# Sets of matmuls on TensorE added behind the last sum of squares of a two-layer encoder kernel

## The chip, the core and the metric

The kernel runs on one core of a Trainium2 chip. The metric is the device time of one execution in microseconds (us), taken as the median of several runs. A profile of one execution gives the span from its first to its last instruction and, for each engine, its instructions in order of time: TensorE (PE in the rows, with its weight loads as PEld), VectorE (DVE), ScalarE (ACT), GpSimd (POOL) and SyncE (SP), whose queue issues nearly all transfers.

## What is computed

The reference is a two-layer encoder trunk on 256 tokens of width 2048. Cut to what matters here:

```python
for i in range(DEPTH):
    h = rmsnorm(x, g_mix[i]);  z = h @ w_in[i]
    ...                                   # two kinds of attention, eight heads each
    x = x + merged @ w_out[i]
    gate, up = jnp.split(rmsnorm(x, g_ffn[i]) @ w_gate_up[i], 2, axis=-1)
    x = x + (jax.nn.silu(gate) * up) @ w_down[i]
    e = p[i] @ w_ple_in[i]
    x = x + jax.nn.sigmoid(rmsnorm(x, g_ple[i]) @ w_ple_gate[i]) * e
return rmsnorm(x, g_final)
```

## The kernel before

The activations lie in the on-chip memory (SBUF) as `xT`: 128 partitions by 16 column blocks by 256 tokens, float32. A product with a weight matrix is made one column block of 128 outputs at a time. Each operand stands as two parts of reduced precision, a high and a low one: an activation block `u` is one tile of 512 columns, the high part in columns 0 to 255 and the low part in 256 to 511 (`ua` and `ub`, sixteen such tiles each), and a piece of weights is two tiles `whi` and `wlo` of up to 1024 columns, that is eight blocks of 128 by 128.

`piece` (L181) loads a piece of weights by a transfer on SP's queue into `w`, copies it to `whi` on ACT, and subtracts on DVE to get `wlo`. There are four buffers of `w` and three of `whi` and of `wlo`. `emit` (L211 and L212) then issues, for each of the blocks, a pair of matmuls with the weights as the stationary operand: the high weights against all 512 columns, and the low weights against the 256 high columns:

```python
PE.matmul(acc, hi[:, s], u, start=start, stop=False)                  # L211
PE.matmul(acc[:, T:], lo[:, s], u[:, :T], start=False, stop=stop)     # L212
```

A product runs over one or more pieces into one bank of the accumulator memory (PSUM). Four banks rotate for products (`ps_mm`), two for attention scores, and two (`ps_at`) for small things. Of the small things three matter below. `turned` makes four transposes of 128 by 128 in float32 by matmuls with an identity (L359). `norm` sums squares over the partitions by float32 matmuls whose moving operand is a single column of ones (L271). `spread` lays the two resulting scales out over the partitions by one float32 matmul of 256 columns (L280). The last column block of the whole kernel's last product uses a variant with three matmuls of 256 columns for each block (L207 to L209).

Where the weights lie matters for the change, so it is said here in bytes within a partition, read modulo 512, which is the length of one block's row of weights: the tiles `ua`, `ub` and `wlo` start at 128, and `whi` starts at 192, behind a 64-byte tile `step` that is only there to move it. So in the kernel before the low weights lie 0 bytes, and the high weights 64 bytes, past the place of the moving operand.

The order on each engine comes from a scheduler that lists instructions by the order of the program where their inputs allow it, with some orders pinned by hand (`keep_in_program_order` pins an instruction behind the one traced before it on its engine). At the end of the last layer, `R = spread(norm(sums, DM), copied=False)` makes the final scales in a bank of `ps_at`; six multiplications on DVE then scale `xT` in place, and six transfers on SP's queue (L704) write the output. Right at the start, eight matmuls of ones into a bank that is never read (L407) run ahead of the real work.

Of the kernel before, what the change touches and what calls it, by code (L numbers as in the profile page):

```python
# [13 lines left out]
F32R = mybir.dt.float32r  # L14
I32 = mybir.dt.int32
AF = mybir.ActivationFunctionType
# [3 lines left out]
P = 128  # L20
T = 256
# [15 lines left out]
PT = 8  # L37
# [15 lines left out]
def encoder(ctx, tc, x, p, positions, cols, lams, wq, wk, wv, wcq, wckv, wkr, wga, wgb,  # L53
            w_q_up, w_kn, w_v, w_bd, w_bm, w_out, w_gate, w_up, w_down, w_pin, w_pg, rope_c, out):
    nc = tc.nc
    V, A, PE = nc.vector, nc.scalar, nc.tensor
# [3 lines left out]
    wts = pool("wts")  # L60
    tmp = pool("tmp")
    stat = pool("stat")
    ps_mm = pool("ps_mm", 4, space=PSUM)
# [3 lines left out]
    def scratch(tag, bufs, n=T):  # L67
        return tmp.tile([P, n], F32, tag=tag, name=tag, bufs=bufs)

    def bank(ps=ps_at, tag="at", name="at", shape=(P, 2 * T)):  # L70
        return ps.tile(list(shape), F32, tag=tag, name=name)

    def tt(o, a, b, op):
        return V.tensor_tensor(out=o, in0=a, in1=b, op=op)  # L74
# [4 lines left out]
    def ts(o, a, s1, s2, op0, op1=ALU.bypass):  # L79
        return V.tensor_scalar(out=o, in0=a, scalar1=s1, scalar2=s2, op0=op0, op1=op1)  # L80


    ua = [const.tile([P, 2 * T], F32R, name=f"ua{j}") for j in range(NC)]
# [12 lines left out]
    xT = const.tile([P, NC, T], F32, name="xT")  # L96
# [4 lines left out]
    at = 0  # L101
# [8 lines left out]
    ident = const.tile([P, P], F32, name="ident")  # L110
    make_identity(nc, ident)
    ones = const.tile([P, P], F32, name="ones")
# [2 lines left out]
    aside = [fa(j) for j in range(5)]  # L115
    posi = aside[0][:, 0, :].bitcast(I32)
    posf = aside[0][:, 1, :]

    def tables():
        V.tensor_copy(posf, posi)  # L120
        got = []
        for i, name in enumerate("pm"):
            ang, k, r, a = (aside[j + i][:, m, :] for j in (1, 3) for m in range(2))
            ts(ang, posf, rc[:, 2 * i : 2 * i + 1], None, ALU.mult)
            ts(k, ang, 1.0 / TWO_PI, ROUND, ALU.mult, ALU.add)
            ts(k, k, ROUND, None, ALU.subtract)
            stt(r, k, -C1, ang, ALU.mult, ALU.add)
            stt(r, k, -C2, r, ALU.mult, ALU.add)
            stt(r, k, -C3, r, ALU.mult, ALU.add)
            ts(r, r, PI_IN, -PI_IN, ALU.min, ALU.max)  # L130
            stt(a, r, -1.0, r, ALU.mult, ALU.min)
            ts(a, a, math.pi / 2, None, ALU.add)
            cs = const.tile([P, T], F32, name="cos_" + name)
            sn = const.tile([P, T], F32, name="sin_" + name)
            A.activation(cs, a, AF.Sin)
            A.activation(sn, r, AF.Sin)
            ts(sn, sn, rc[:, 2 * i + 1 : 2 * i + 2], None, ALU.mult)
            got += [cs, sn]
        return got
# [74 lines left out]
    def product(src, us, whole=False):  # L214


        acc = bank(ps_mm, "mm", "mm")
        n = len(us)
        for a in range(0, n, PT):
            m = min(PT, n - a)  # L220
            hi, lo = piece(src[:, a * P : (a + m) * P], m)
            emit(acc, hi, lo, 0, us[a : a + m], a == 0, a + m == n, whole)
        return acc[:, :T] if whole else acc
# [10 lines left out]
    def joined(acc, o=None):  # L234
        t = scratch("join", 3)
        A.activation(t, acc[:, T:], AF.Copy)  # L236
        o = scratch("a", 4) if o is None else o
        tt(o, acc[:, :T], t, ALU.add)
        return o
# [7 lines left out]
    def rsqrt(src, n, eps, width):  # L247

        v, y, a = (stat.tile([P, 2 * DH], F32, tag="r" + s, name="r" + s, bufs=2)[:, :width] for s in "vya")
        ts(v, src, 1.0 / n, eps, ALU.mult, ALU.add)  # L250
        ts(y.bitcast(I32), v.bitcast(I32), -0.5, 1597463007.0, ALU.mult, ALU.add)
        for _ in range(3):
            stt(a, y, -0.5, y, ALU.mult, ALU.mult)
            tt(a, a, v, ALU.mult)
            stt(y, a, 1.5, y, ALU.add, ALU.mult)
        return y

    def square_into(acc, src, first):
        if first:
            A.activation(acc, src, AF.Square)  # L260
        else:
            sq = scratch("sq", 2)
            A.activation(sq, src, AF.Square)  # L263
            tt(acc, acc, sq, ALU.add)

    def norm(sums, n):

        s = bank()
        for j, a in enumerate(sums):
            for b in range(2):  # L270
                PE.matmul(s[:, b : b + 1], a[:, b * P : (b + 1) * P], ones[:, 0:1], start=j + b == 0, stop=j + b == len(sums))  # L271
        return rsqrt(s[:, 0:2], n, EPS, 2)

    def spread(col, copied=True):

        dg = stat.tile([P, 2, P], F32, tag="dg", name="dg", bufs=1)
        for b in range(2):
            ts(dg[:, b, :], ident, col[:, b : b + 1], None, ALU.mult)
        s = bank()
        PE.matmul(s[:, :T], ones, dg, start=True, stop=True)  # L280
        if not copied:
            return s[:, :T]
        row = stat.tile([P, T], F32, tag="row", name="row", bufs=2)
        A.activation(row, s[:, :T], AF.Copy)  # L284
        return row

    def normed(sums, one, two):

        got = [joined(one())]
        col = norm(sums, DM)  # L290
        got.append(joined(two()))
        return spread(col), col, got

    def squares():
        return stat.tile([P, T], F32, tag="ssq", name="ssq", bufs=2)

    def stream(us, gain):

        acc = squares()

        def add(c):
            split(us[c], xT[:, c, :], g(gain, c))
            square_into(acc, xT[:, c, :], c == 0)

        return acc, add
# [110 lines left out]
    for L in range(DEPTH):  # L416

        steps = values(wv[L], ua, None if L else load)
        for vd in steps:
            if L == 0 and vd is not None:  # L420
# [3 lines left out]
                with after_splits():  # L424
                    rcol = norm([sq0[0][:, j, :] for j in range(2)], DM)
                    next(steps)
                    R = spread(rcol)
                    cos_p, sin_p, cos_m, sin_m = tables()
                    lambdas()
                break  # L430
            if L:
                next(steps)
                rcol = norm([acc], DM)
                next(steps)
                R = spread(rcol)
                break
# [5 lines left out]
        for o, t in ((cr, cos_p), (sr, sin_p), (crm, cos_m), (srm, sin_m)):  # L442
            tt(o, t, R, ALU.mult)

# [17 lines left out]
        def latent(us, w, raws):  # L462
            ss = squares()
            for c in range(len(us)):
                tt(raws[c], joined(product(w[L, c], ua)), R, ALU.mult)
                square_into(ss, raws[c], c == 0)
# [55 lines left out]
        def gate(w, store, n):  # L522
            tt(store(n), joined(product(w[L, n], ua)), R, ALU.mult)

# [115 lines left out]
        acc, add = stream(ub, f"g_ffn{L}")  # L640
# [4 lines left out]

        R, _, pre = normed([acc], lambda: product(w_gate[L, 0], ub), lambda: product(w_up[L, 0], ub))
        pT, es = ua[14:], []
# [4 lines left out]
        for part, (f0, f1) in enumerate(FF_PARTS):  # L652
            for f in range(f0, f1):
                a = pre.pop(0) if pre else joined(product(w_gate[L, f], ub))
# [9 lines left out]
            if last:  # L664
                acc, add = stream(ub, f"g_ple{L}")
# [12 lines left out]
        if final:  # L678
            sums = [squares(), squares()]
# [5 lines left out]
        else:  # L685
            acc, add = stream(ua, f"g_mix{L + 1}")
        for n in range(NC):
            if final and n == NC - 1:
                a = scratch("a", 4)
                tt(a, product(w_pg[L, n], ub, True), R, ALU.mult)  # L690
            else:
                a = pre.pop(0) if pre else joined(product(w_pg[L, n], ub))
# [5 lines left out]
            add(n)  # L698

    R = spread(norm(sums, DM), copied=False)  # L700
    for n, m in ((0, 1), (1, 1), (2, 2), (4, 4), (8, 4), (12, 4)):
        o = xT[:, n : n + m, :]
        tt(o, o, R[:, None, :].to_broadcast([P, m, T]), ALU.mult)
        nc.sync.dma_start(out[:, n : n + m, :], o)  # L704
# [84 lines left out]
```

## Time and profile before

| what | us |
|---|---|
| two timed runs | 2911.41 and 2915.62 |
| their median | 2913.51 |
| the profiled execution's own time | 2910.11 |
| its span, first to last instruction | 2908.3 |
| TensorE busy within the span | 2890.7 |
| weight loads busy (beside the matmuls) | 2539.6 |
| VectorE busy | 2062.3 |
| ScalarE busy | 1524.6 |

The mean granted TensorE clock was 0.998 of full speed. In the rows, a matmul's own duration contains time in which the next one already streams, so what a matmul costs is read from the distance between the starts of successive ones, or from a stretch's length divided by the count of instructions in it. A float32 matmul that isn't a transpose leaves two records, one of the reduced type (`fp32r`, which the rows also print as f32) leaves one. Times in windows and timelines count from the start of the span.

### The profile page before, as it was taken

How to read it: one execution, taken by the hardware profiler on the slowest of the kernel's cores; microseconds unless marked ns; L12 is line 12 of the kernel's file. 1: busy time of each engine (PE TensorE's matmuls, PEld its weight loads, DVE VectorE, ACT ScalarE, POOL GpSimd, SP SyncE). 2: the span in 40 equal slices, each digit the busy share in tenths (PEclk: the TensorE clock that was granted, in tenths of full speed). 3: DMA queues.
4: the chain of work that ended last, by engine and by line, in shares of the span. 5: the costliest groups of instructions: out<-in, count | busy, mean ns of one | idle time of the engine just before them, and what ended most of it. 6: DMA issues, size and time to landing. Idle time of an engine off the chain costs nothing.

```text
span 2908.3 us, 43980 instructions
## 1 busy us (share of the span) xinstructions
PE 2890.7 (99%) x16750; PEld 2539.6 (87%) x16750; DVE 2062.3 (71%) x3529; ACT 1524.6 (52%) x2529; POOL 1.7 (0%) x9
## 2 busy tenths in 40 slices
PE   9999999999999999999999999999999999999998
PEld 7888888888888888888888888888888888888887
DVE  7897658776666666667859976687666666666676
ACT  6676545554444444454646755555444444444554
POOL 0000000000000000000000000000000000000000
PEclk9999999999999999999999999999999999999999
DMA  7554466555665566566565445666556655655664
GB/s 236 165 163 147 159 195 197 190 186 188 184 193 189 183 189 192 189 188 188 189 188 168 151 153 167 195 195 189 186 188 184 193 188 180 197 188 189 189 186 141
DMA packets 156019, 532.40 MB, mean 183 GB/s; under 512 B 16928, under 2 KB 23840, under 8 KB 155808
## 3 DMA queue, kind: packets, MB, share of 16 engines
q1 hardware_dynamic: 155376, 529.01, 57.9%
q8 instruction: 131, 2.15, 0.3%
q14 instruction: 80, 0.66, 0.1%
q10 hardware_dynamic: 432, 0.59, 0.1%
HBM read 527.43 MB, written 2.10 MB: 182 GB/s over the span
## 4 chain that ended last, share of the span: by engine, by line
PE 99%; DVE 1%; ACT 0%; DMA 0%; SPq 0%; issue 0%; DVEq 0%
PE mm L211 61%; PE mm L212 31%; PE S L341 1%; PE mmv L394 1%; PE mmv L392 1%; PE mmv L393 1%; PE at L359 0%; PE at L563 0%; PE at L620 0%; DMA w<-in_wv 0%; PE at L280 0%; DVE xT L74 0%; PE at L271 0%; DVE wlo L74 0%; ACT whi L181 0%; DVE a L74 0%
## 5 line engine op out<-in xcount | busy, mean ns | idle before, releaser
L181 ACT ACTIVATE whi<-w 128x1024 fp32r<-128x1024 f32 (+2 forms) x1029 | 1068.5, 1039 | 1311.4 <-issue 749.3
L74 DVE TENSOR_TENSOR wlo<-w,whi 128x1024 fp32r<-128x1024 f32 (+2 forms) x1029 | 1228.6, 1194 | 740.2 <-ACT whi L181 730.4
L211 PE MATMUL mm<-ub,whi 128*128 128x512 f32 x3952 | 1381.5, 394 | 0.0
L211 PE MATMUL mm<-ua,whi 128*128 128x512 f32 x3744 | 1307.8, 394 | 0.0
L212 PE MATMUL mm<-ub,wlo 128*128 128x256 f32 x3952 | 1107.7, 280 | 0.0
L212 PE MATMUL mm<-ua,wlo 128*128 128x256 f32 x3744 | 1048.5, 280 | 0.0
L211 PEld LDWEIGHTS mm<-ub,whi 128*128 128x128 f32 x3952 | 742.1, 188 | 164.5
L211 PEld LDWEIGHTS mm<-ua,whi 128*128 128x128 f32 x3744 | 702.5, 188 | 151.5
L212 PEld LDWEIGHTS mm<-ub,wlo 128*128 128x128 f32 x3952 | 749.0, 190 | 0.8
L212 PEld LDWEIGHTS mm<-ua,wlo 128*128 128x128 f32 x3744 | 708.2, 189 | 2.2 <-DVE wlo L74 0.4
L74 DVE TENSOR_TENSOR a<-mm,join 128x256 f32<-128x256 f32 x421 | 174.8, 416 | 0.3 <-ACT join L236 0.2
L236 ACT ACTIVATE join<-mm 128x256 f32<-128x256 f32 x453 | 165.9, 367 | 5.4 <-PE mm L212 5.0
L74 DVE TENSOR_TENSOR xT<-xT,mm 128x256 f32<-128x256 f32 x256 | 106.6, 419 | 48.4 <-PE mm L212 44.5
L74 DVE TENSOR_TENSOR a<-a,row 128x256 f32<-128x256 f32 x207 | 87.2, 424 | 6.6 <-ACT row L284 0.8
L74 DVE TENSOR_TENSOR a<-a 128x256 f32<-128x256 f32 x120 | 51.0, 425 | 4.0
L392 PE MATMUL mmv<-whi,ua 128*128 128x512 f32 x128 | 51.0, 399 | 2.0 <-ACT whi L181 2.0
L74 DVE TENSOR_TENSOR ua<-a,ua 128x256 fp32r<-128x256 f32 x120 | 50.1, 417 | 1.0 <-ACT ua L244 1.0
L393 PE MATMUL mmv<-whi,ua 128*128 128x512 f32 x128 | 50.5, 395 | 0.0
L244 ACT ACTIVATE ua<-a 128x256 fp32r<-128x256 f32 x120 | 48.2, 402 | 2.7 <-DVE a L74 2.6
L350 ACT ACTIVATE E<-S,nm 128x256 f32<-128x256 f32 x96 | 44.2, 470 | 5.1 <-DVE nm L80 5.0
L394 PE MATMUL mmv<-wlo,ua 128*128 128x512 f32 x128 | 46.8, 397 | 0.1
L74 DVE TENSOR_TENSOR ssq<-ssq,sq 128x256 f32<-128x256 f32 x97 | 40.5, 417 | 0.5 <-ACT sq L263 0.5
(154 smaller groups left out, 1158.9 us busy)
## 6 DMA issues: line engine op xcount, KB each, us to landing
w<-in_w_gate SPq DMA_DIRECT2D x176, 512.0 KB, 4.6
w<-in_w_up SPq DMA_DIRECT2D x176, 512.0 KB, 4.5
w<-in_w_down SPq DMA_DIRECT2D x128, 512.0 KB, 3.7
w<-in_wga SPq DMA_DIRECT2D x64, 512.0 KB, 3.8
w<-in_wgb SPq DMA_DIRECT2D x64, 512.0 KB, 4.5
w<-in_w_out SPq DMA_DIRECT2D x64, 512.0 KB, 4.2
w<-in_w_pg SPq DMA_DIRECT2D x64, 512.0 KB, 4.4
w<-in_w_down SPq DMA_DIRECT2D x64, 384.0 KB, 3.6
```

Of the source, the lines that this page charges most:

```text
L74: return V.tensor_tensor(out=o, in0=a, in1=b, op=op)
L181: last_split[:] = A.activation(hi[:, :m], w[:, :m], AF.Copy), tt(lo[:, :m], w[:, :m], hi[:, :m].bitcast(F32), ALU.subtract)
L211: PE.matmul(acc, hi[:, s], u, start=start, stop=False)
L212: PE.matmul(acc[:, T:], lo[:, s], u[:, :T], start=False, stop=stop)
L236: A.activation(t, acc[:, T:], AF.Copy)
L244: return A.activation(hi, src, AF.Copy), tt(lo, src, hi.bitcast(F32), ALU.subtract)
L341: PE.matmul(S[:, b, :], q[:, b * P : (b + 1) * P], k, start=j == 0, stop=j == len(pairs) - 1)
L350: last_exp[0] = A.activation(E[:, b, :], S[:, b, :], AF.Exp, bias=nm[:, b : b + 1], scale=scale, accum_out=sm[:, b : b + 1])
L392: PE.matmul(banks[b], xh, hi[:, s], start=a + j == 0, stop=False)
L393: PE.matmul(banks[b], xl, hi[:, s], start=False, stop=False)
L394: last_mm[:] = [PE.matmul(banks[b], xh, lo[:, s], start=False, stop=a + j == n - 1)]
```

## The change

A function `others` is added and called once, behind the last `spread` and ahead of the six multiplications that make the output. It copies the first 1024 columns of `xT` into one `whi` and one `wlo` buffer on ACT (names `sh` and `sl`). Then it runs over 64 pairs of places: eight for the high and eight for the low part, in steps of 16 elements, 64 bytes. The index is turned by one for the high part, so that `h` and `l` count the distance from the moving operand's place in steps of 64 bytes for both; `h = 1, l = 0` is the pair of places that the kernel before has. At each pair of places it runs four sets of seven pairs of matmuls in the form of L211 and L212, each into a bank that is never read, and each behind one of four kinds of other matmuls, into a bank that isn't read either:

- `quarters`: five matmuls of 256 columns with low weights
- `transposes`: four float32 transposes of 128 by 128 of `xT`
- `sums`: four float32 matmuls of one column, with `xT` as the stationary operand
- `couples`: two matmuls of 512 columns with the high weights, then two of 256 with the low ones

All these matmuls are pinned in program order on TensorE. Nothing is removed. The buffers come from the tags that are there already, so no tile of the kernel before moves.

```diff
+    def others():
+        src = xT[:, :4, :].rearrange("p c t -> p (c t)")
+        sh = wts.tile([P, PT * P], F32R, tag="whi", name="side", bufs=3)
+        sl = wts.tile([P, PT * P], F32R, tag="wlo", name="side", bufs=3)
+        for t in (sh, sl):
+            A.activation(t, src, AF.Copy)
+        keep = tc.keep_in_program_order
+        mm = lambda *a, **k: keep(PE.matmul(*a, **k))
+
+        def quarters(at, h, l):
+            for j in range(5):
+                mm(at[:, :T], sl[:, j * P : (j + 1) * P], ua[j][:, :T], start=j == 0, stop=j == 4)
+
+        def transposes(at, h, l):
+            for j in range(4):
+                keep(PE.transpose(at[:, j * P : (j + 1) * P], xT[:, j, :P], ident))
+
+        def sums(at, h, l):
+            for j in range(4):
+                mm(at[:, j : j + 1], xT[:, j, :P], ones[:, 0:1], start=True, stop=True)
+
+        def couples(at, h, l):
+            for j in range(2):
+                mm(at, sh[:, h + j * P : h + (j + 1) * P], ua[j], start=j == 0, stop=False)
+            for j in range(2):
+                mm(at[:, T:], sl[:, l + j * P : l + (j + 1) * P], ua[j][:, :T], start=False, stop=j == 1)
+
+        for h in range(8):
+            for l in range(8):
+                name = "w" + chr(97 + h) + chr(97 + l)
+                oh, ol = 16 * ((h - 1) % 8), 16 * l
+                for before in (quarters, transposes, sums, couples):
+                    before(bank(name="between"), oh, ol)
+                    acc = bank(ps_mm, "mm", name)
+                    for j in range(7):
+                        mm(acc, sh[:, oh + j * P : oh + (j + 1) * P], ua[j], start=j == 0, stop=False)
+                        mm(acc[:, T:], sl[:, ol + j * P : ol + (j + 1) * P], ua[j][:, :T], start=False, stop=j == 6)
...
     R = spread(norm(sums, DM), copied=False)
+    others()
     for n, m in ((0, 1), (1, 1), (2, 2), (4, 4), (8, 4), (12, 4)):
```

## The prediction

> **What bounds the kernel now.** I read the page's busy shares first, then its chain of work that ended last, then windows over long stretches, then the timeline of the last 20 us.
>
> ```profile
> span 2908.3 us, 43980 instructions
> PE 2890.7 (99%) x16750; PEld 2539.6 (87%) x16750; DVE 2062.3 (71%) x3529; ACT 1524.6 (52%) x2529; POOL 1.7 (0%) x9
> ...
> PE 99%; DVE 1%; ACT 0%; DMA 0%; SPq 0%; issue 0%; DVEq 0%
> ```
>
> TensorE is busy for 2890.7 of 2908.3 us, and the chain is TensorE for 99% of the span. All idle time of TensorE is 17.6 us, so matmuls that are added go onto the path at their full price, wherever they are put. Everything then hangs on the price of one pair, and that I take from stretches in which nothing but pairs run:
>
> ```profile
> 360.00:480.00 120.00, 120.00 (x708) 106.13 (x707) 81.66 (x119) 61.61 (x96) 0.00 (x0) 1.00 0.62 196
> 2200.00:2800.00 600.00, 600.00 (x3431) 527.84 (x3430) 398.16 (x585) 282.32 (x398) 0.00 (x0) 1.00 0.61 188
> ```
>
> These are windows; the second and third numbers are the length and TensorE's busy time, with the matmuls counted behind it. In the later one 600 us hold 3431 matmuls, half of them of 512 and half of 256 columns: 600 / 1715.5 = 0.3497 us a pair. In the earlier one it is 120 / 354 = 0.339 us, of the same form with its weights at the same places. So a pair has more than one speed. The timeline shows a third, behind four transposes:
>
> ```profile
> 327.58 0.60 PE L359 MATMUL at<-ident,E 128*128 128x128 f32 x4
> 327.94 0.48 PE L211 MATMUL mm<-ua,whi 128*128 128x512 f32 x1
> 328.25 0.28 PE L212 MATMUL mm<-ua,wlo 128*128 128x256 f32 x1
> 328.38 0.40 PE L211 MATMUL mm<-ua,whi 128*128 128x512 f32 x1
> 328.61 0.28 PE L212 MATMUL mm<-ua,wlo 128*128 128x256 f32 x1
> ...
> 333.32 0.40 PE L211 MATMUL mm<-ua,whi 128*128 128x512 f32 x1
> ```
>
> From the pair that starts at 328.38 to the one at 333.32 there are 14 pairs: 4.94 / 14 = 0.353 us. Same places, three prices, 0.339, 0.350 and 0.353; the speed stays with a run of pairs, and changes where other matmuls come between.
>
> **The change part by part.**
>
> **The sets.** 64 places, four sets, seven pairs: 1792 pairs. `couples` is two more pairs at each place in another order, 128. Together 1920 pairs at 0.3497 = 671.4 us. I take 0.3497 since it lies between the other two and is the mean of the longest stretch. The trace has only one pair of places for this form; for the other 63 the nearest rows are matmuls of other operands, whose weights and moving operand lie at the same place:
>
> ```profile
> 312.45 0.52 PE L341 MATMUL S<-fb,fa 128*128 128x256 f32 x3
> 312.81 0.52 PE L341 MATMUL S<-kr,fc 128*128 128x256 f32 x3
> ```
>
> Three of 256 columns in 0.36 us (312.45 to 312.81) are 0.120 each. A pair is 768 columns, three times as many: 0.360 us. So the bounds of a pair's mean over all places are 0.340 (671.4 - 18.6) and 0.360 (671.4 + 19.8).
>
> By the Trainium skill (TensorE: Matmul & The Clock Gate, section Back-to-back issue gap) a warm matmul costs N / 2.4 + 2.5 ns, 215.8 and 109.2, so 0.325 us for a pair: an estimate of 624 us for the 1920. The stretches above show 0.339 at best, so I go by them.
>
> **What goes between.** `quarters` is five matmuls of 256 columns. The nearest rows are the last product's, which has only such matmuls:
>
> ```profile
> 2892.03 0.28 PE L209 MATMUL mm<-ub,wlo 128*128 128x256 f32 x1
> ...
> 2892.38 0.28 PE L209 MATMUL mm<-ub,wlo 128*128 128x256 f32 x1
> ```
>
> From 2892.03 to 2892.38 there are three (L209, L207, L208): 0.1175 each with rounding, 320 of them 37.6 us (0.113 to 0.120 by the pairs' speeds: 36 to 38).
>
> `transposes`: in the rows of 327.58 four transposes, and what the next matmul loses, take until the start of its L212 at 328.25, 0.67 us, against 0.235 for a plain L211 step (328.38 to 328.61). So they cost 0.44, and 64 times that is 28.2 us (up to 0.49 each, 31, with rounding and one slower step).
>
> `sums`: four float32 matmuls of one column, as in `norm`:
>
> ```profile
> L271 PE MATMUL at<-ones,ssq x44: 164/250/271, 87.4 to 2895.3; 128*128 128x1 f32 x44
> L271 PE MATMUL at<-ones,fb x8: 166/250/250, 44.6 to 45.2; 128*128 128x1 f32 x8
> ```
> ```profile
> 2808.63 0.50 PE L271 MATMUL at<-ones,ssq 128*128 128x1 f32 x4
> 2808.99 0.47 PE L211 MATMUL mm<-ub,whi 128*128 128x512 f32 x1
> 2809.30 0.28 PE L212 MATMUL mm<-ub,wlo 128*128 128x256 f32 x1
> ```
>
> The 26 such matmuls of the kernel before leave 52 records (44 and 8), two each. Four records with what follows take 0.67 - 0.235 = 0.435 us, 0.11 a record. Eight take 0.88, 64 times 56.3 us. Were they one record each, 28 us would be saved; the count of records speaks against it.
>
> **The start.** The tail of the kernel before:
>
> ```profile
> 2894.97 0.51 ACT L683 ACTIVATE xT<-xT,gcol 128x256 f32<-128x256 f32 x1
> ...
> 2898.33 1.22 PE L280 MATMUL at<-dg,ones 128*128 128x256 f32 x2 [2.73 <-DVE dg L80]
> 2899.59 4.74 DVE L74 TENSOR_TENSOR xT<-xT,at 128x256 f32<-128x256 f32 x6 [1.32 <-PE at L280]
> 2900.04 4.65 SPq L704 DMA_DIRECT2D out_y<-xT  x6
> ```
> ```profile
> 2897.00:2898.00 1.00, 0.00 (x0) 0.00 (x0) 0.85 (x6) 0.00 (x0) 0.00 (x0) 0.50 0.00 0
> ```
>
> The granted clock (the 0.50 ahead of the last two columns of the window) has fallen to half by then, since TensorE idles around the last norm. So the added matmuls start at half speed. How long that lasts shows at the kernel's start:
>
> ```profile
> 1.05 3.78 PE L407 MATMUL at<-ones 128*128 128x128 f32 x16 [1.05 <-DVE ones L113]
> 5.17 0.61 PE L393 MATMUL mmv<-whi,ua 128*128 128x512 f32 x1
> 5.60 0.41 PE L392 MATMUL mmv<-whi,ua 128*128 128x512 f32 x1
> ```
>
> From 1.05 to about 5.6 they take twice as long, then 0.41: some 4.5 us at half speed, which lose 2.3 us.
>
> ```profile
> L181 ACT ACTIVATE whi<-w 128x1024 fp32r<-128x1024 f32 x939 | 998.0, 1063 | 1193.9 <-issue 732.9 <-PE mm L211 346.4 <-ACT sq L263 64.2
> ```
>
> The two added ACT copies take 1.06 each (1063 ns, by the `whi` copies of the same shape). ACT is done at 2895.48 and the first added matmul follows the one at 2898.33, so 2.1 us are covered; were they queued ahead of a weight copy instead, up to 2 us would show on TensorE.
>
> **The end.** The change adds a wait: the multiplications that overwrite blocks 0 to 3 of `xT` must come behind the last transposes and `sums` that read them. If the other multiplications queue behind these on DVE, and their six transfers on SP's queue, the output chain (2899.59 to 2908.3, 8.7 us) starts when the last `sums` end. Two sets and `couples` still follow then, 16 pairs, 5.6 us. So the span ends about 3 us behind the last matmul. If only the first four blocks wait it is less, but not below about 1 us, which the closing instructions take.
>
> **The sum.** 671.4 + 37.6 + 28.2 + 56.3 + 2.3 = 795.8 us on TensorE. The last matmul of before ends at 2898.33 + 1.22 = 2899.55, so now at 3695.4, and the span at 3698.5. The profiled execution of before took 2910.11, 1.8 more than its span: 3700.3. It lies 3.4 under the median of the runs; against that median the forecast is 3703.7, so 3704.
>
> **The rivals.**
>
> *The places clash.* If at some places the weight load and the moving stream get in each other's way more than the rows above show, the mean leaves the bounds. A price by rows, which are groups of the page's kind with the mean ns of one:
>
> ```profile
> L211 PEld LDWEIGHTS mm<-ub,whi 128*128 128x128 f32 x3952 | 742.1, 188 | 164.5
> L212 PEld LDWEIGHTS mm<-ub,wlo 128*128 128x128 f32 x3952 | 749.0, 190 | 0.8
> ```
>
> The two weight loads of a pair take 0.188 and 0.190 us and overlap each other in part. If they no longer did, a pair would take 0.378 and the 1920 pairs 54 us more: 3758. For it speaks that one and the same form already runs at three speeds at one pair of places. Against it, the matmuls of other operands (L341, L207) stay at 0.120 or below for 256 columns.
>
> The Trainium skill (same page, section Step-by-step: what each phase is for) says that loading the next weights doesn't take read bandwidth from the running matmul, because the two have separate read ports; by that places would not matter at all. The three speeds above at the same places say that something does, and no row shows what.
>
> *The pairs stream freely.* In the added stretch no transfer, no DVE and no ACT work runs. If these were what holds a pair at 0.35, it would run as a stream without other work does. The nearest rows are a float32 `spread`, two records of 256 columns that count double:
>
> ```profile
> 627.73 0.60 PE L280 MATMUL at<-dg,ones 128*128 128x256 f32 x2
> 627.97 0.58 PE L211 MATMUL mm<-ub,whi 128*128 128x512 f32 x1
> 628.39 0.28 PE L212 MATMUL mm<-ub,wlo 128*128 128x256 f32 x1
> ```
>
> Both records take 0.66 less a plain L211 step of 0.23 (328.38 to 328.61), 0.215 each. As the price of 512 columns that gives 0.3225 for a pair and 0.1075 for 256 columns: 3704 - 1920 x 0.0272 - 320 x 0.010 = 3649.
>
> ```profile
> 2888.00:2892.00 4.00, 4.00 (x36) 4.00 (x35) 1.95 (x5) 1.62 (x4) 0.00 (x0) 1.00 0.00 0
> 2892.70 0.42 DVE L74 TENSOR_TENSOR a<-mm,row 128x256 f32<-128x256 f32 x1 [2.08 <-PE mm L209]
> ```
>
> Against it, around 2892 no transfer runs (the last two numbers of the window's row), DVE sits idle (2.08 us ahead of the row at 2892.70), and 256 columns still take 0.117.
>
> The skill's gap above would give nearly the same time by its own figures, an estimate of 3654.
>
> *Not slower.* Matmuls whose results nobody reads could be dropped ahead of the run, or take no time. Then the time would be 2913.5. Deciding is whether at least 737 of the 795.8 us vanish, since 2% is 58 us. Against it: the warm-up matmuls at the start (L407, in the row at 1.05) are eight float32 matmuls that nobody reads, and their 16 records are there.
>
> **How the numbers follow.** The forecast's case (means from 0.340 to 0.360 a pair): 0.74, with a range of its own of 3680 to 3731 (bounds of the pairs, of `transposes`, of the start and end). Clash: 0.19. Free streaming: 0.06. Not slower: 0.01. The range goes to 3758, so that it takes in the clash up to its price, and leaves the free case out. Slower by over 2% (about what a measurement can tell from no change) 0.99; the rest is the last case, within 2% 0.008 and faster by over 2% 0.002.
>
> **What would show it.** The added matmuls' records: 256 sets, whose seven pairs last 2.38 to 2.52 us each; the granted clock at half in the first 5 us of them; eight records for each `sums`; the last multiplication behind the last `sums`. Wrong would be a set at some places of 2.6 us or more, or sets whose speed doesn't depend on what ran before them.

## The result, and the profile after

The changed kernel takes 3701.64 us (median of 3701.21 and 3702.07), against 2913.51 before: a ratio of 1.2705, 95% interval 1.265 to 1.276. The forecast was 3704, with a range of 3680 to 3758.

The page of the changed kernel, its busy shares, its chain, and three groups. In a group the last numbers are busy us, mean ns of one, and the idle time ahead of it with what ended it:

```profile
span 3699.4 us, 53839 instructions
PE 3686.7 (100%) x21678; PEld 3252.8 (88%) x21678; DVE 2063.8 (56%) x3529; ACT 1526.7 (41%) x2531; POOL 1.7 (0%) x9
...
PE 99%; DVE 0%; ACT 0%; DMA 0%; SPq 0%; issue 0%
...
L252 PE MATMUL mm<-ub,whi 128*128 128x512 f32 x3952 | 1381.5, 394 | 0.0
L253 PE MATMUL mm<-ub,wlo 128*128 128x256 f32 x3952 | 1107.7, 280 | 0.0
L74 DVE TENSOR_TENSOR xT<-xT,at 128x1024 f32<-128x1024 f32 (+2 forms) x6 | 4.8, 862 | 790.6 <-PE between L129 790.6
```

TensorE has 4928 records more: 3840 of the 1920 pairs, 320 of `quarters`, 256 of `transposes` and 512 of `sums`. So nothing was left out, and the 256 float32 matmuls of `sums` do leave two records each. The old pairs (now at L252 and L253, since the added lines shift the numbers by 41) have the busy time that they had: 1381.5 and 1107.7 us with `ub`. The multiplications of the output waited 790.6 us for the added reads.

The start of the added stretch in the timeline (`waa` are the sets of `h = 0, l = 0`, `x14` a set of seven pairs), and the granted clock over it, ahead of the last two columns:

```profile
2899.01 1.22 PE L321 MATMUL at<-dg,ones 128*128 128x256 f32 x2 [2.74 <-DVE dg L80]
2899.67 1.63 PE L129 MATMUL between<-ua,side 128*128 128x256 f32 x5
2901.09 4.07 PE L129 MATMUL waa<-ua,side 128*128 128x512 f32 x14
2905.01 0.60 PE L137 MATMUL between<-ident,xT 128*128 128x128 f32 x4
2905.36 2.72 PE L129 MATMUL waa<-ua,side 128*128 128x512 f32 x14
2907.92 0.95 PE L129 MATMUL between<-ones,xT 128*128 128x1 f32 x8
```
```profile
2899.00:2901.00 2.00, 1.99 (x7) 1.81 (x8) 0.00 (x0) 0.00 (x0) 0.00 (x0) 0.50 0.00 0
2901.00:2903.00 2.00, 2.00 (x8) 1.71 (x8) 0.00 (x0) 0.00 (x0) 0.00 (x0) 0.50 0.00 0
2903.00:2905.00 2.00, 2.00 (x10) 1.72 (x9) 0.00 (x0) 0.00 (x0) 0.00 (x0) 0.67 0.00 0
2905.00:2907.00 2.00, 2.00 (x15) 1.82 (x14) 0.00 (x0) 0.00 (x0) 0.00 (x0) 1.00 0.00 0
2912.00:3690.00 778.00, 778.00 (x4834) 696.64 (x4834) 0.49 (x2) 0.00 (x0) 0.00 (x0) 1.00 0.00 1
```

The first `quarters` take 1.42 us and the first set 3.92; later ones take about 0.6 and 2.5. The clock is at half for some 4.6 us. Then TensorE is busy without a gap, at full clock, with ACT idle and next to nothing on DVE and in the transfers. The two added copies ran on ACT before that, from 2887.6 to 2889.9; matmuls of the old products ahead of them and behind them lie alike, 0.67 us later than in the kernel before, so the copies cost TensorE nothing that the rows show.

The end, with the last `sums`, the output's multiplications, and the transfers:

```profile
3689.78 0.36 PE L129 MATMUL between<-ones,xT 128*128 128x1 f32 x2
3689.84 4.41 DVE L74 TENSOR_TENSOR xT<-xT,at 128x256 f32<-128x256 f32 x5
3689.95 4.67 SPq L746 DMA_DIRECT2D out_y<-xT  x6
3690.00 2.69 PE L129 MATMUL whh<-ua,side 128*128 128x512 f32 x14
3692.53 0.85 PE L129 MATMUL between<-ua,side 128*128 128x512 f32 x4
3693.22 2.62 PE L129 MATMUL whh<-ua,side 128*128 128x512 f32 x14
```

All six transfers go out behind the last `sums`, and the span ends at 3699.4, about 3.6 us behind the last matmul.

**Speeds by place.** From the starts of each set's matmuls I worked out the ns of a pair over its last four pairs. Over the 255 sets at full clock (all but the first) they lie between 340.0 and 355.3, with a mean of 348.8; by what ran before them 348.3 (`quarters`), 349.1 (`transposes`), 348.6 (`sums`) and 349.4 (`couples`). Four places in the order of these kinds:

| place | quarters | transposes | sums | couples |
|---|---|---|---|---|
| h = 1, l = 0 (the kernel before) | 350.0 | 350.0 | 349.5 | 350.0 |
| h = 1, l = 1 | 353.2 | 353.2 | 351.0 | 353.5 |
| h = 2, l = 0 | 352.5 | 351.8 | 352.2 | 352.2 |
| h = 3, l = 0 | 340.0 | 340.0 | 343.0 | 341.2 |

`h = 7` gives what `h = 3` gives, and `l = 4` often what `l = 0` gives: the pattern comes again after 256 bytes, exactly for `h` in most rows and with exceptions for `l`. Only `h = 3` and `7` with `l = 0` and `4` are near 341 behind all four kinds.

### The profile page after: what moved, and what is told of

The parts are those of the page before. It is cut to its first block, busy times and chain, and to the rows that moved or that the text cites. A ratio compares the mean times of both kernels' runs of the same rounds, so it can differ in the third digit from the quotient of the medians.

```text
span 3699.4 us, 53839 instructions
## 1 busy us (share of the span) xinstructions
PE 3686.7 (100%) x21678; PEld 3252.8 (88%) x21678; DVE 2063.8 (56%) x3529; ACT 1526.7 (41%) x2531; POOL 1.7 (0%) x9
## 4 chain that ended last, share of the span: by engine, by line
PE 99%; DVE 0%; ACT 0%; DMA 0%; SPq 0%; issue 0%
PE mm L252 48%; PE mm L253 24%; PE between L129 4%; PE S L382 1%; PE mmv L435 1%; PE mmv L433 1%; PE mmv L434 1%; PE between L137 1%; PE at L400 0%; PE at L604 0%; PE at L661 0%; PE waa L129 0%; PE wff L129 0%; PE wbf L129 0%; PE wfb L129 0%; PE wbb L129 0%
## 5 line engine op out<-in xcount | busy, mean ns | idle before, releaser
L252 PE MATMUL mm<-ub,whi 128*128 128x512 f32 x3952 | 1381.5, 394 | 0.0
L252 PE MATMUL mm<-ua,whi 128*128 128x512 f32 x3744 | 1308.0, 394 | 0.0
L253 PE MATMUL mm<-ub,wlo 128*128 128x256 f32 x3952 | 1107.7, 280 | 0.0
L253 PE MATMUL mm<-ua,wlo 128*128 128x256 f32 x3744 | 1048.5, 280 | 0.0
L252 PEld LDWEIGHTS mm<-ub,whi 128*128 128x128 f32 x3952 | 742.1, 188 | 164.0
L252 PEld LDWEIGHTS mm<-ua,whi 128*128 128x128 f32 x3744 | 702.5, 188 | 151.8
L253 PEld LDWEIGHTS mm<-ub,wlo 128*128 128x128 f32 x3952 | 748.9, 190 | 0.8
L253 PEld LDWEIGHTS mm<-ua,wlo 128*128 128x128 f32 x3744 | 708.1, 189 | 2.2 <-DVE wlo L74 0.4
L74 DVE TENSOR_TENSOR xT<-xT,at 128x1024 f32<-128x1024 f32 (+2 forms) x6 | 4.8, 862 | 790.6 <-PE between L129 790.6
L74 DVE TENSOR_TENSOR xT<-xT,mm 128x256 f32<-128x256 f32 x256 | 106.8, 420 | 48.4 <-PE mm L253 44.6
L129 PE MATMUL between<-ua,side 128*128 128x256 f32 (+1 forms) x576 | 104.5, 308 | 0.0
L129 PEld LDWEIGHTS between<-ua,side 128*128 128x128 f32 x576 | 86.8, 190 | 11.2
L129 PEld LDWEIGHTS between<-ones,xT 128*128 128x128 f32 x512 | 62.5, 191 | 2.8
L129 PE MATMUL between<-ones,xT 128*128 128x1 f32 x512 | 60.7, 240 | 0.0
L433 PE MATMUL mmv<-whi,ua 128*128 128x512 f32 x128 | 51.0, 400 | 2.3 <-ACT whi L222 2.1
```

The source lines that it names most:

```text
L129: mm = lambda *a, **k: keep(PE.matmul(*a, **k))
L433: PE.matmul(banks[b], xh, hi[:, s], start=a + j == 0, stop=False)
```

## The experiments

The first two ask whether a place's speed in these short sets is its speed in the kernel. `STEP` is the length, in elements, of the small tile ahead of the high weights.

**`step48`**

```diff
-STEP = 16
+STEP = 48
```

Expected: 

> The kernel before without the added sets; its 64-byte tile ahead of the high weights is made 192 bytes long, so that they lie 192 bytes past the moving operand's place (h = 3, l = 0). Theory 1, that the place sets a pair's speed: the added sets showed 340, 340, 343 and 341 ns a pair at these places behind the four kinds, and 350, 350, 350 and 350 at those of before (h = 1, l = 0). The 7696 pairs of the kernel before took 348.7 ns in the mean, so 341 would save 7696 x 7.7 ns = 59 us: about 2854 us, with nearly all pairs at 340 to 343 ns. Rival, that the pairs' speed is a matter of what ran before them alone, so that a place shows only in these short sets: no change, 2913 us, pairs at 349 ns.

Measured: 2866.26 us against 2911.28 for the kernel before on the same chip, ratio 0.9846 (0.9832 to 0.9859). So the place counts in the kernel too. But 12 us of the expected gain are missing. Two windows of this kernel:

```profile
630.00:760.00 130.00, 130.00 (x745) 113.94 (x744) 87.07 (x128) 62.95 (x94) 0.00 (x0) 1.00 0.55 186
2200.00:2600.00 400.00, 400.00 (x2355) 353.89 (x2354) 270.06 (x393) 189.71 (x266) 0.00 (x0) 1.00 0.60 195
```

From 2200 a pair takes 400 / 1177.5 = 0.340 us, from 630 it takes 130 / 372.5 = 0.349. Counted over the kernel, some 1600 pairs ran at about 350 ns, most of them in four stretches at a norm: 423 and 236 pairs in the first layer, 423 and 219 in the second. The place `h = 3, l = 0` has two speeds. The two stretches of 423 begin right behind the norm's `spread`. The other two are slow already 24 pairs ahead of it, behind the one-column matmuls of the same norm; the steps from one high matmul to the next are 0.34 us ahead of these and 0.35 behind them:

```profile
1344.00 0.39 PE L211 MATMUL mm<-ub,whi 128*128 128x512 f32 x1
...
1344.34 0.39 PE L211 MATMUL mm<-ub,whi 128*128 128x512 f32 x1
...
1344.68 0.50 PE L271 MATMUL at<-ones,ssq 128*128 128x1 f32 x4
...
1345.48 0.40 PE L211 MATMUL mm<-ub,whi 128*128 128x512 f32 x1
...
1345.83 0.40 PE L211 MATMUL mm<-ub,whi 128*128 128x512 f32 x1
```

**`step32`**, the same with `STEP = 32`. Expected: 

> The kernel before with its 64-byte tile made 128 bytes long (h = 2, l = 0). The added sets showed 352.5, 351.8, 352.2 and 352.2 ns a pair there. Theory 1 (place): 7696 x 3.4 ns = 26 us more than before, about 2940 us. Rival (what ran before, or that the old place was bad and any move helps): 2913 us, or less.

Measured: 2940.94 us, ratio 1.0102 (1.0088 to 1.0115). A window of it, for the one of `step48` from 2200:

```profile
2200.00:2600.00 400.00, 400.00 (x2274) 349.34 (x2273) 259.65 (x379) 181.65 (x252) 0.00 (x0) 1.00 0.59 187
```

That is 400 / 1137 = 0.352 us a pair, as in the added sets; single pairs go from 346 to 359 ns by turns. Moving the high weights makes the kernel 30 us slower here, 26 expected. The rival, that any move helps, is out.

**`sets_alone`**

```diff
-                    before(bank(name="between"), oh, ol)
```

It leaves out the matmuls between the sets. Expected: 

> The changed kernel without the four kinds of other matmuls between the sets; at each pair of places 28 pairs run without a break. By the sum of terms: 3701.6 less 38.3 (quarters), 28.3 (transposes), 57.3 (sums) and 44.6 (couples) = 3533 us. If the kinds between them set a pair's speed, the four sets of one place should now be alike, and whole places at 340 ns or at 353 ns appear, with the mean anywhere from 340 to 353: 3516 to 3539 us. Rival, that the place alone does: each place keeps the mean that it had over the four kinds, 349.7 ns over all, within 1 ns.

Measured: 3530.19 us. The four kinds together are worth 171.4 us, 168.5 by the terms. Now the 28 pairs of a place run on end:

```profile
3136.40 9.68 PE L129 MATMUL wda<-ua,side 128*128 128x512 f32 x56
3145.92 9.87 PE L129 MATMUL wdb<-ua,side 128*128 128x512 f32 x56
...
3175.23 9.96 PE L129 MATMUL wde<-ua,side 128*128 128x512 f32 x56
3185.02 2.16 PE L129 MATMUL wdf<-ua,side 128*128 128x512 f32 x11
```

From start to start, `wda` (`h = 3, l = 0`) takes 9.52 / 28 = 0.340 us a pair and `wde` (`h = 3, l = 4`) 9.79 / 28 = 0.350; the latter had 340 to 343 ns in the changed kernel. In the other direction `h = 1, l = 0` runs at 340 ns here, where it had 350. So a place doesn't keep its mean, and the rival is out: what ran before decides which of its speeds a place takes, and the run of pairs keeps it. The speeds are few: over the last 20 steps of their 28 pairs, 36 of the 63 places behind the first settle within 0.2 ns of 340.0, 346.7 or 350.0, and the others lie from 350.9 to 353.6.

**`moved`**

```diff
-        for t in (sh, sl):
+        mov = wts.tile([P, PT * P], F32R, tag="w32", name="mov", bufs=W_BUFS)
+        for t in (sh, sl, mov):
             A.activation(t, src, AF.Copy)
+        u = mov[:, 16 : 16 + 2 * T]
...
-                oh, ol = 16 * ((h - 1) % 8), 16 * l
+                oh, ol = 16 * h, 16 * ((l + 1) % 8)
```

with `u` for `ua[j]` in the sets, `quarters` and `couples`, and the weights of `quarters` moved along. Expected: 

> The changed kernel with the sets' moving operand taken from a copy that lies 64 bytes further, and with both weights' offsets turned so that the letters h and l still count from the moving operand's place. (All moving operands of the sets are now one tile; quarters are moved with it.) If the distance to the moving operand is what counts, the table of speeds by h, l and kind is that of the changed kernel, cell by cell, within 1 ns. Rival, that the weights' own address counts (or their distance to each other alone): the table is that of the changed kernel turned by one in h and in l, so that the 340 ns cells (h = 3 and 7 with l = 0 and 4) turn up under h = 2 and 6 with l = 7 and 3. The time is about 3702 us either way.

Measured: 3701.55 us. Of 255 cells, 73% are within 1 ns of the changed kernel's; of the table turned by one either way, 22% and 17%, and two cells of the table drawn at random agree so in 25%. By what ran before it is 92% behind `quarters`, 86% behind `couples`, 53% behind `transposes` and 61% behind `sums`. So it is the distance to the moving operand that counts, and not the weights' own address; but not in every cell, though I had expected it in all. The two kinds with the low shares are those that were not moved along, so the distance between them and the sets did change; that this is why is an argument, not a run. The run also makes one tile the moving operand of all pairs, which the changed kernel doesn't. The cells `h = 3, l = 0` behind `sums` and `couples` went from 343 and 341 to 350.

**`half_step`**

```diff
-                oh, ol = 16 * ((h - 1) % 8), 16 * l
+                oh, ol = 16 * ((h - 1) % 8) + 8, 16 * l + 8
```

Expected: 

> The changed kernel with both weights' offsets 32 bytes further in every set (the moving operand and the four kinds stay). If the places count by lines of 64 bytes, the table of speeds stays as it was to within 3 ns, and 340 ns shows at h = 3 and 7 with l = 0 and 4. If the distance counts more finely, other cells come out, some of them outside 340 to 355 ns. The time is 3702 us within 10 either way.

Measured: 3701.18 us; 36% of the cells within 1 ns (25% would be by chance), changes of up to 14 ns, and no cell at 340 any more: 343.3 to 354.0, mean 349.3. So a shift of 32 bytes counts. Whether it counts as a finer distance, or because a block of weights then lies otherwise on lines of 64 bytes, this run doesn't tell apart; since the kinds between were not moved along, part of the change may also be what ran before. The mean hardly moves.

**`no_read_xT`**

```diff
-                keep(PE.transpose(at[:, j * P : (j + 1) * P], xT[:, j, :P], ident))
+                keep(PE.transpose(at[:, j * P : (j + 1) * P], ub[j].bitcast(F32)[:, :P], ident))
...
-                mm(at[:, j : j + 1], xT[:, j, :P], ones[:, 0:1], start=True, stop=True)
+                mm(at[:, j : j + 1], ub[j].bitcast(F32)[:, :P], ones[:, 0:1], start=True, stop=True)
```

Expected: 

> The changed kernel with transposes and sums reading other tiles (at the same place modulo 512) in place of the first blocks of the result, so that the output's multiplications needn't wait for them. Theory of the end: the output leaves at the start of the added stretch, and the span ends about 1 us behind the last matmul in place of 3.6 us: about 3697 us of span against 3699.4, all of it at the end. Rival, that the closing time hangs on TensorE's last matmul and not on the output: 3699.4.

Measured: a span of 3696.0 us, and 3697.81 us of time. The timeline of this kernel:

```profile
2898.72 1.22 PE L321 MATMUL at<-dg,ones 128*128 128x256 f32 x2 [2.73 <-DVE dg L80]
2899.38 1.63 PE L129 MATMUL between<-ua,side 128*128 128x256 f32 x5
2899.97 4.74 DVE L74 TENSOR_TENSOR xT<-xT,at 128x256 f32<-128x256 f32 x6 [1.31 <-PE at L321]
2900.42 4.66 SPq L746 DMA_DIRECT2D out_y<-xT  x6
...
3692.58 2.62 PE L129 MATMUL whh<-ua,side 128*128 128x512 f32 x14
```

The output leaves 790 us earlier, and the span ends 0.8 us behind the last matmul (3692.58 + 2.62) in place of 3.6. Its first added matmul lies 0.3 us earlier too, and its last one ends 0.6 earlier (3695.20 for 3695.84), so 2.8 of the 3.4 us are the end's. All 255 speeds are the same as in the changed kernel to 0.3 ns: the speeds are no chance of a run.

The next four look for what keeps `step48` at 350 ns in places.

**`step48_kick`**

```diff
-        return spread(col), col, got
+        row = spread(col)
+        at = bank(name="kick")
+        for j in range(5):
+            tc.keep_in_program_order(PE.matmul(at[:, :T], ub[j][:, T : T + P], ub[j][:, :T], start=j == 0, stop=j == 4))
+        return row, col, got
```

Expected: 

> The kernel with the 192-byte tile (h = 3, l = 0), with five unread matmuls of 256 columns behind the spread of each of the four norms of the model's width that go ahead of long products (20 matmuls in all, at about 0.12 us: 2.4 us). In the run without them, 1627 pairs were slow (350 ns), among them 423 and 236 behind such a spread in the first layer and 423 and 219 in the second, 1301 together. Theory 2, that what runs before a run of pairs picks one of the speeds that a place has, and that the pairs keep it: behind five matmuls of 256 columns the added sets always ran at 340 ns here, so these 1301 pairs go to 340 as well and save 13 us less 2.4: about 2856 us. Rival, that these stretches are slow for what they contain: no gain, 2866 + 2.4 = 2869 us, the same 1301 pairs at 350 ns.

Measured: 2868.83 us, ratio 0.9858 (0.9842 to 0.9875), with the stretches of 423, 236, 423 and 219 pairs at 350 ns as before. The theory's expectation fell: five matmuls of 256 columns, behind which the sets had run at 340, change nothing here. (In the stretches of 236 and 219 they came when the pairs already ran at 350.) But in `step48` itself the stretch of 423 pairs ends at a place that can be seen:

```profile
769.31 0.40 PE L211 MATMUL mm<-ua,whi 128*128 128x512 f32 x1
769.55 0.28 PE L212 MATMUL mm<-ua,wlo 128*128 128x256 f32 x1
769.66 0.62 PE L211 MATMUL mm<-ua,whi 128*128 128x512 f32 x2
770.12 0.40 PE L212 MATMUL mm<-ua,wlo 128*128 128x256 f32 x2
770.36 0.39 PE L211 MATMUL mm<-ua,whi 128*128 128x512 f32 x1
770.59 0.28 PE L212 MATMUL mm<-ua,wlo 128*128 128x256 f32 x1
770.70 0.39 PE L211 MATMUL mm<-ua,whi 128*128 128x512 f32 x1
```

Where two products meet, the scheduler has put two high and two low matmuls behind each other; ahead of it a pair takes 0.35, behind it 0.34. The kernel before has such couples too, and there they go both ways: within three pairs, those at 775.86 and 2216.91 lead from 350 ns to 340, and those at 529.22 and 1970.27 from 340 to 350.

**`step48_couple`** and **`couple_only`** give the first two blocks of each piece that order, with `STEP` 48 and 16:

```diff
+                low = lambda s=s, u=u, stop=stop: PE.matmul(acc[:, T:], lo[:, s], u[:, :T], start=False, stop=stop)
-                PE.matmul(acc[:, T:], lo[:, s], u[:, :T], start=False, stop=stop)
+                if j == 0 and len(us) > 1:
+                    later.append(low)
+                else:
+                    for do in (*later, low):
+                        do()
+                    later.clear()
```

Expected of the first: 

> The kernel with the 192-byte tile (h = 3, l = 0), with the first two blocks of each piece issued as high, high, low, low. In the 192-byte run the slow stretch of 423 pairs behind a norm's spread ended exactly where the scheduler had by chance put two high and two low matmuls behind each other (at 769.66), and 340 ns followed to its end. Theory 2 in its present form, that the pairs keep a speed until the order of weight loads is broken, and that two couples in that order lead to 340 ns at this place: the 1627 slow pairs shrink to a few hundred, and 10 to 15 us go: 2851 to 2856 us. Rival, that the slow stretches are a matter of their contents, or that the end at 769.66 was chance: no gain, 2866 us; or a loss, since at other places couples kept 350 ns (the moved sets at h = 3, l = 0): up to 7696 x 9.5 ns, 2930 us.

Measured: 2883.05 us, ratio 0.9905 (0.989 to 0.9919), 17 us more than `step48`. No stretch of more than 13 pairs near 350 is left, but behind each couple some three pairs are slower: of 5535 pairs outside the couples 2718 took about 340, 901 about 345, 878 about 346.5 and 1000 from 350 to 352 ns. These cost more than the long stretches had.

Expected of the second: 

> The same order of the first two blocks in the kernel before, with its 64-byte tile (h = 1, l = 0). Behind couples the added sets ran at 350 ns there (348 and 352 in turn). Theory 2, with place and what went before both counting: no gain, pairs at 350 throughout in place of 348.7 and the fast stretches (340 ns) gone: up to 10 us more, 2911 to 2922 us. Rival, that the order helps by itself wherever the weights lie: 10 us or more less than before.

Measured: 2919.8 us, ratio 1.0031 (1.0018 to 1.0044), 9 us more, with nearly all pairs from 348 to 353 ns and the stretches at 340 gone. So the order in every piece costs time at both places; here it leaves hardly any at 340, at `h = 3` about half of them.

**`step48_once`** has `STEP = 48` and a couple in four products alone, `couple=f == 2` in the product with `w_gate` and `couple=n == 3` in that with `w_pg`. Expected: 

> The kernel with the 192-byte tile (h = 3, l = 0) and the high, high, low, low order in only four places: the first two blocks of the first product that starts behind the spread of each of the four norms of the model's width. With that order in every piece, the long stretches behind these spreads ran at 340 ns again between the couples, but each couple cost some three slower pairs. Theory 2: one couple turns the stretch to 340 ns and it stays there; of the 1301 slow pairs some 1250 go from 350 to 340: 12 us, about 2854 us, with the slow pairs down to some 400. Rival, that a couple's effect is lost again within the stretch: 2862 to 2866 us.

Measured: 2859.21 us, ratio 0.9821 (0.9808 to 0.9835), the fastest version found. The couple of the up and gate products in the timeline, and the rest of that stretch as a window:

```profile
626.80 0.40 PE L212 MATMUL mm<-ub,whi 128*128 128x512 f32 x1
627.03 0.28 PE L213 MATMUL mm<-ub,wlo 128*128 128x256 f32 x1
627.15 0.62 PE L212 MATMUL mm<-ub,whi 128*128 128x512 f32 x2
627.61 0.40 PE L213 MATMUL mm<-ub,wlo 128*128 128x256 f32 x2
627.84 0.39 PE L212 MATMUL mm<-ub,whi 128*128 128x512 f32 x1
```
```profile
628.00:760.00 132.00, 132.00 (x779) 116.71 (x778) 91.61 (x136) 65.48 (x99) 0.00 (x0) 1.00 0.59 192
```

132 / 389.5 = 0.339 us a pair, where `step48` had 0.349. The two stretches of 423 are down to 15 pairs each. But the 236 and 219 pairs of the other products stayed at 350 (234 and 217).

**`step48_later`** moves that second couple one product on (`couple=n == 4`). Expected: 

> As the run before, but in the gate product behind the last spread of each layer the couple comes one product later. There the couple had followed the spread after three pairs and left the pairs at 350 ns (234 and 217 slow pairs); in the up and gate products it had come 14 pairs behind the spread and turned them to 340. If it is the settled 350 ns run that a couple turns, these 451 pairs shrink to some 40 and 4 us more go: 2855 us. If a couple can't turn these stretches at all: 2859 us.

Measured: 2859.89 us, ratio 0.9821 (0.9808 to 0.9835), with 234 and 217 pairs at 350 as before. A couple doesn't turn these, even 20 pairs behind the spread. The pairs ahead of the couple don't show which stretch will turn: with steps from one start to the next of 233 ns for a high and 117 for a low matmul, the stretch at 627.15 of `step48_once` turned and those at 1351.97 and 2768.04 stayed; with 232 and 118, the one at 2043.16 turned and the two of `step48_later` stayed. The difference shows only in the couple itself, which runs 234, 226, 114, 121 ns, within 1 ns, where it turns the stretch and 233, 241, 120, 116 where it doesn't. The stretches that stay are the ones that were slow ahead of the `spread`, behind the one-column matmuls. That this is the reason is not shown.

## Why the prediction was right, point by point

| term | forecast, us | measured, us |
|---|---|---|
| 1792 pairs in sets, at full clock | 626.7 | 625.2 |
| `couples`, 128 pairs | 44.8 | 44.6 |
| `quarters` | 37.6 | 38.3 |
| `transposes` | 28.2 | 28.3 |
| `sums` | 56.3 | 57.3 |
| half clock at the start | 2.3 | 2.4 |
| from the last matmul to the end of the span | 3 | 3.6 |

The measured terms are worked out from the starts of the matmuls in the trace, each kind with what the first high matmul behind it loses.

*All of it goes onto the path.* Right: TensorE was full before, and its added records lie on end, 796.2 us from the first start to the last end, for 795.8.

*0.3497 us a pair.* Right: 0.3488 over all the sets' last pairs. It was the speed of the longest stretch at one pair of places, and that the mean over 64 places came out near it was luck: the places by themselves differ from 341 to 353 ns. The bounds of 0.340 and 0.360, from the fastest stretch and from matmuls of other operands, held every one of the 255 sets, not only the mean.

*The start and the wait at the end.* Right, shown by the clock's rows and by `no_read_xT`. The forecast that the span ends 3 us behind the last matmul because the output queues behind the last `sums` is the one term tested by taking it away.

*The small errors.* The stretch ahead of the added matmuls came out 0.7 us longer, with its `spread` at 2899.01 for 2898.33; 0.6 of it is there by 628 us, and the first products begin 0.4 us later, so most of it isn't the added work. The forecast let the added matmuls begin at the end of that `spread`, 1.22 us behind its start; they began 0.66 behind it. These two errors cancel by luck. The median lies 2.2 us over the span here; the forecast had taken 1.8 and 3.4 on top of it.

*The rivals.* Clash: no set came to 0.360, let alone 0.378. That places do matter was in it, and is right by 12 ns from the fastest place to the slowest in this form. As to the Trainium skill (TensorE: Matmul & The Clock Gate, section Step-by-step: what each phase is for), which lets the loading of weights take no read bandwidth from the running matmul: `step48` and `step32` differ only in where the high weights lie (and the tiles behind them), by 74.7 us, so the place matters, in whatever way. No run shows in which.

Free streaming: out. From 2912 to 3690 nothing else ran, and a pair still took 0.349. The gap of N / 2.4 + 2.5 ns in the Trainium skill (the same page, section Back-to-back issue gap), an estimate of 0.325 a pair, isn't reached by any run of pairs here; 0.340 is the least. That section gives it for a single matmul, which the forecast didn't say.

Not slower: out, by the count of records.

*What would be wrong.* The forecast said that sets whose speed doesn't depend on what ran before them would speak against it. They do depend: `sets_alone` shows it at the same places. The sign of 2.38 to 2.52 us a set was drawn too narrowly: by the rows the sets at full clock last 2.38 to 2.57, since behind `transposes` and `sums` the first high matmul carries a loss that the forecast had booked with these. None reached 2.6. What was only a guess is how the speed depends on what ran before. The theory that five matmuls or a couple set the speed at a place fell in `step48_kick` and, in part, in `step48_later`.

*What stays open.* Which of a place's speeds a run of pairs takes. It came again to 0.3 ns in a second run of the same sets, it follows from what went before, it lasts for hundreds of pairs, and a changed order of two blocks ends some stretches of 350 ns and not others. Why these give way and those don't isn't settled.

## What to carry to other kernels

When work goes onto an engine that is full, price it by the length of a stretch in which only that form runs, divided by its count, and take the bounds from the fastest and the slowest rows of the same size. Where a stream of like matmuls shows two speeds, look for the place of the stationary operand against the moving one, and try other places in the kernel itself: a tile of 192 bytes in place of 64 was worth 1.5%, and an added couple in four products brought it to 1.8%. Behind an in-place result, ask what still reads it, since a read that nobody needs can hold the output back.

## What the runs showed of the hardware that was not expected

- The speed of a pair of matmuls of 512 and 256 columns depends on where the weights lie against the moving operand, with a pattern that mostly comes again after 256 bytes and changes with a shift of 32: 340 to 355 ns.
- One and the same place has several speeds, and a run of pairs keeps the one that it has settled on: in the kernels with `STEP` 16, 32 and 48 no unbroken run of 16 pairs or more changes it, the longest over 1422 pairs (at 350 ns in the kernel before, at 340 in `step48`). Over two runs of the same sets all 255 speeds agreed to 0.3 ns.
- Two high and two low matmuls behind each other turned two stretches of 423 pairs from 350 to 340 ns (`step48_once`, against `step48`) and left two others of 236 and 219 pairs at 350.
